# One step of a two-way recurrence: both directions through each stage together

## The chip, the cores and the metric

The kernel runs on one core of a Trainium2 chip. The metric is the device time of one execution in microseconds. Before the change it is 4082.77 us, the median of three runs (4077.72 to 4091.49).

PE is the matmul engine, PEld its weight loads, DVE the vector engine, ACT the scalar engine, POOL the GpSimd engine and SP the engine that issues most DMAs. Each engine runs its instructions in the order in which they stand in its queue.

## What is computed

One encoder layer over 2304 tokens (256 of a prompt and 2048 of a sample, width 1024): a norm, one input projection, then side by side a recurrent head group (RWKV-7, 8 heads of width 64, run forwards and backwards) and an attention group (8 query heads on 2 key/value heads), an output projection, a SwiGLU FFN and a last norm, all in 32-bit floats. The part that matters here is the recurrence. With a state S of 64x64 per head it is, per token:

```python
def step(S, inp):
    r_t, w_t, k_t, v_t, a_t, b_t = inp
    sa = jnp.einsum('bhvk,bhk->bhv', S, a_t)
    S = S * w_t[:, :, None, :] + sa[..., None] * b_t[:, :, None, :] + v_t[..., None] * k_t[:, :, None, :]
    return S, jnp.einsum('bhvk,bhk->bhv', S, r_t)
```

It is run once in the order of the tokens and once against it (`reverse=True`), with decay and gates of their own, and the two outputs are added and normalised per head.

## The kernel before

The tokens are cut into 36 chunks of 64. Within a chunk the recurrence is turned into matrix products; only the state passes from chunk to chunk. The forward direction (d = 0) takes the chunks upwards while the backward one (d = 1) takes them downwards, so one *step* of the scan treats two chunks, one per direction. There are 36 steps: 32 for the sample, 4 for the prompt.

A step has two parts, written as generators.

`scan_prep` (L626) loads a chunk's operands, forms the Gram products (L657) in two PSUM tiles of tag `g` (there are two such banks), masks them into `cl` and `mrb` on DVE (L661, L663), and transposes `bk` (L668) with an eviction on ACT (L669).

`scan_chain` (L686) is the serial part of one direction and one chunk. Its four stages write one half, `hb[:, d]`, of a single PSUM bank `hb`:
- first stage (L705): product of `cl` with `sv`, which holds state and v; ACT evicts it into `ry` (L707);
- second stage (L711): product with the inverse `x`; ACT evicts it in two copies into `sav` (L712, L713);
- third stage (L717): the change of the state; DVE adds the old state (L720) and multiplies by the decay `wc` (L722); then `scan_sv` copies the new state into the next `sv`, one half on ACT (L681), one on POOL (L682);
- fourth stage (L730, L733): the output product, into the same half of `hb`. In the first half of the steps ACT copies it out (L737) and a DMA stores it; in the second half DVE adds the stored output of the other direction (L746), and every second chunk `scan_out` normalises a tile of 128 tokens.

`scan` (L794) starts the preparation of the next step together with the chains of this one and takes a turn of each generator in every round. In the rounds it also advances the triangular inverses (`back`), and `build` advances attention by 2.75 units per round (`RATE_S`). A unit of attention is a score product (L880, L881) with its maximum on DVE (L882) and exponential on ACT (L884), or four transposes (L913) with evictions on ACT and DVE (L175, L181) and two products with the values (L916, L917). POOL multiplies the exponentials by their factors (L901), sixteen tiles in a row, each time that all scores of a tile of queries are there.

The text gives priorities, not the order: a scheduler places each instruction in its engine's queue when, by its own timeline, the operands and a buffer are ready, those earlier in the text first. So the queue of PE holds the chain's groups of eight heads between attention's products, and which stand next to each other is not written anywhere in the code. Two PE instructions are issued for each product of 32-bit operands in the chain, so eight heads are sixteen instructions. A product of attention that is 512 wide is one.

`e_dir` (L463 to L467), which runs before the scan, stores the decay at the end of each chunk in `wc[d]`, at the chunk's own number.

Of the kernel before, what the change touches and what calls it, by code (L numbers as in the profile page):

```python
# [8 lines left out]
F32 = mybir.dt.float32  # L9
# [8 lines left out]
P = 128  # L18
# [78 lines left out]
class Kern:  # L97
# [308 lines left out]
    def e_dir(self, e, p, d):  # L406
# [52 lines left out]
        for c in range(nch):  # L459
            for h in range(2):  # L460
# [5 lines left out]
        pool.tensor_scalar(out=self.wc[d][:, p, ch0:ch0 + nch], in0=e1[:, :nch, 64 - 64 * d], scalar1=1.0, scalar2=0.0,  # L466
                           op0=ALU.mult, op1=ALU.add)  # L467
# [156 lines left out]
    def scan_prep(self, d, c, sb, ps):  # L624

        nc = self.nc  # L626
        act, dve = nc.scalar, nc.vector
        bi, j = self.blk(c)
        gr, off = BLOCKS[bi][2:]
        cs = slice(j * P, j * P + P)  # L630
        q_ = self.sq = getattr(self, "sq", {})

        def T(tag, shape, bufs):
            return sb.tile(shape, F32, name=tag, tag=tag, bufs=bufs)
        ar = self.ard[d][bi]
        cl = T("cl", [P, 2, 4, P], 4)
        for e in range(2):
            rows = slice(e * 64, e * 64 + 64)
            self.ld(cl[rows, e], ar[:, rows, cs].rearrange("q p t -> p q t"))
        bk = T("bk_", [P, 4, P], 2)  # L640
        self.ld(bk, self.bkd[d][bi][:, :, cs].rearrange("q p t -> p q t"))
        x = T("x_", [P, 4, C], 3)
        for e in range(2):
            self.ld(x[e * 64:e * 64 + 64], self.xd[d][gr][:, e, off + j].rearrange("q s t -> s q t"))
        sav = T("sav", [P, 4, 2, C], 3)
        v = self.vtd[bi][j * C:(j + 1) * C, :]
        self.ld(sav[64:128].rearrange("p q e c -> p (q e c)"), v)
        gm = self.c["gmask_" + "fb"[d]]
        mrb = T("mrb", [C, 4, 2, C], 4)
        bkt = T("bkt", [P, 4, P], 3)  # L650
        q_[d, c] = dict(cl=cl, x=x, sav=sav, mrb=mrb, bkt=bkt, v=v.rearrange("t (q e c) -> t q e c", e=2, c=C))
        yield
        psgs = [ps.tile([P, 4, P], F32, name="g", tag="g", bufs=2) for _ in range(2)]
        for q in range(4):
            for e in range(2):
                rows = slice(e * 64, e * 64 + 64)
                nc.tensor.matmul(psgs[e][:, q, :], bk[rows, q, :], cl[rows, e, q, :], start=True, stop=True)  # L657
        for e in range(2):
            other = slice(64 - e * 64, 128 - e * 64)
            psg = psgs[e]  # L660
            dve.tensor_tensor(out=cl[other, e], in0=psg[64:128], op=ALU.mult,  # L661
                              in1=gm[64:128].rearrange("p (o t) -> p o t", o=1).broadcast_to([64, 4, P]))
            dve.tensor_tensor(out=mrb[:, :, e, :], in0=psg[0:64, :, 64:128], op=ALU.mult,  # L663
                              in1=gm[0:64, 64:128].rearrange("p (o t) -> p o t", o=1).broadcast_to([64, 4, C]))
            yield
        psg = ps.tile([P, 4, P], F32, name="g", tag="g", bufs=2)
        for q in range(4):
            nc.tensor.transpose(psg[:, q, :], bk[:, q, :], self.ident)  # L668
        act.copy(out=bkt, in_=psg)  # L669
        yield  # L670

    def scan_sv(self, d, c, st, sb):

        sv = sb.tile([P, 4, 2, C], F32, name="sv", tag=f"sv{d}", bufs=2)
        v = self.sq[d, c]["v"]
        self.ld(sv[64:128, :, 0, :], v[:, :, 0, :])
        self.ld(sv[0:64, :, 1, :], v[:, :, 1, :])
        if st[0] is None:
            st[0] = sb.tile([P, 4, C], F32, name="sc", tag=f"sc{d}", bufs=2)
            self.nc.gpsimd.memset(st[0], 0.0)  # L680
        self.nc.scalar.copy(out=sv[0:64, :, 0, :], in_=st[0][0:64])  # L681
        self.nc.gpsimd.tensor_scalar(out=sv[64:128, :, 1, :], in0=st[0][64:128], scalar1=1.0, scalar2=0.0, op0=ALU.mult,  # L682
                                     op1=ALU.add)
        st[1] = sv

    def scan_chain(self, d, c, nxt, st, first, sb, ps):  # L686
# [3 lines left out]
        o = self.sq[d, c]  # L690
        cl, x, sav, mrb, bkt = (o[k] for k in ("cl", "x", "sav", "mrb", "bkt"))

        def T(tag, shape, bufs):
            return sb.tile(shape, F32, name=tag, tag=tag, bufs=bufs)
        if st[1] is None:
            self.scan_sv(d, c, st, sb)
        sv = st[1]
        heads = [(h // 2, h % 2, slice(h % 2 * 64, h % 2 * 64 + 64)) for h in range(8)]

        
        def H():
            return self.hb[:, d]
        psa = H()
        for q, e, rows in heads:
            nc.tensor.matmul(psa[rows, q, :], cl[:, e, q, 0:64], sv[:, q, e, :], start=True, stop=True)  # L705
        ry = T("ry", [P, 4, C], 2)
        act.copy(out=ry, in_=psa)  # L707
        yield
        psx = H()
        for q, e, rows in heads:  # L710
            nc.tensor.matmul(psx[rows, q, :], x[rows, q, :], ry[rows, q, :], start=True, stop=True)  # L711
        act.copy(out=sav[0:64, :, 0, :], in_=psx[0:64])  # L712
        act.copy(out=sav[0:64, :, 1, :], in_=psx[64:128])  # L713
        yield
        pss = H()
# [684 lines left out]
```

## Time and profile before

| | |
|---|---|
| median of three runs | 4082.77 us |
| profiled execution, its own time | 4076.95 us |
| its span | 4074.8 us |
| PE busy | 3880.8 us, 95% |
| DVE busy | 2866.1 us, 70% |
| ACT busy | 2005.5 us, 49% |
| POOL busy | 1257.7 us, 31% |
| scan, first product of the chain to the last | 1015.0 to 2221.8 us |

Busy time is the time in which an engine executes something. PE's matmuls are pipelined, so a row of the time line for PE gives the start of a group, the time to the end of its last matmul, and the number of instructions; the pace is read from one start to the next. In brackets a row names how long the engine was idle before it, and what ended that; "issue" means that nothing in the profile explains it.

### The profile page before, as it was taken

How to read it: one execution, taken by the hardware profiler on the slowest of the kernel's cores; microseconds unless marked ns; L12 is line 12 of the kernel's file. 1: busy time of each engine (PE TensorE's matmuls, PEld its weight loads, DVE VectorE, ACT ScalarE, POOL GpSimd, SP SyncE). 2: the span in 40 equal slices, each digit the busy share in tenths (PEclk: the TensorE clock that was granted, in tenths of full speed). 3: DMA queues.
4: the chain of work that ended last, by engine and by line, in shares of the span. 5: the costliest groups of instructions: out<-in, count | busy, mean ns of one | idle time of the engine just before them, and what ended most of it. 6: DMA issues, size and time to landing. Idle time of an engine off the chain costs nothing.

```text
span 4074.8 us, 71176 instructions
## 1 busy us (share of the span) xinstructions
PE 3880.8 (95%) x26208; PEld 3336.7 (82%) x26208; DVE 2866.1 (70%) x4553; ACT 2005.5 (49%) x3940; POOL 1257.7 (31%) x1776
## 2 busy tenths in 40 slices
PE   8999999979999999999999889999989999999998
PEld 7987878746777777777777689998889988799987
DVE  5478586899889776898887577754477744577643
ACT  4345444456666655656666344443344433344432
POOL 2245353543223556734433122200122200212100
PEclk9999999979999999999999999999999999999999
DMA  6567566662433455444441423243423253422251
GB/s 200 166 204 228 173 207 192 207 165 59 101 74 86 92 120 118 114 109 104 109 111 43 146 86 104 96 181 109 166 93 104 96 184 110 159 87 96 102 181 67
DMA packets 646876, 524.32 MB, mean 129 GB/s; under 512 B 368512, under 2 KB 555520, under 8 KB 646528
## 3 DMA queue, kind: packets, MB, share of 16 engines
q1 hardware_dynamic: 577264, 438.36, 36.2%
q0 software_dynamic: 16944, 68.43, 5.1%
q10 hardware_dynamic: 52320, 12.98, 1.5%
q8 instruction: 207, 3.39, 0.3%
q14 instruction: 141, 1.16, 0.1%
HBM read 355.59 MB, written 166.37 MB: 128 GB/s over the span
## 4 chain that ended last, share of the span: by engine, by line
PE 76%; DVE 9%; DMA 4%; POOL 4%; issue 3%; ACT 3%; SPq 1%; ACTq 0%; DVEq 0%; POOLq 0%
PE acc L1082 23%; PE acc L211 8%; PE acc L212 8%; PE acc L213 8%; PE at L913 5%; PE g L657 3%; PE ao L917 3%; PE ao L916 3%; PE as L880 3%; PE as L881 2%; DVE nm L882 1%; DVE ptl L181 1%; PE hb L705 1%; PE hb L730 1%; PE g L597 1%
## 5 line engine op out<-in xcount | busy, mean ns | idle before, releaser
L1082 PE MATMUL acc<-H,wsh 128*128 128x384 f32 x3168 | 814.6, 337 | 32.6 <-ACT cg L1110 23.0
L1082 PEld LDWEIGHTS acc<-H,wsh 128*128 128x128 f32 x3168 | 578.7, 190 | 36.2 <-ACT cg L1110 24.1
L1082 PE MATMUL acc<-H,wsl 128*128 128x384 f32 x1584 | 533.2, 337 | 0.0
L901 POOL TENSOR_SCALAR p<-p,f 128x512 f32<-128x512 f32 (+1 forms) x528 | 372.8, 728 | 284.8 <-DVE f L897 235.9
L884 ACT ACTIVATE p<-as,nm 128x512 f32<-128x512 f32 (+1 forms) x528 | 360.9, 684 | 162.4 <-DVE nm L882 133.8
L211 PE MATMUL acc<-wsh,H 128*128 128x512 f32 x1080 | 419.8, 391 | 14.6 <-ACT wsh L175 14.6
L212 PE MATMUL acc<-wsl,H 128*128 128x512 f32 x1080 | 420.6, 390 | 0.0
L213 PE MATMUL acc<-wsh,H 128*128 128x512 f32 x1080 | 415.6, 389 | 0.0
L175 ACT CAST pth<-at 128x512 fp32r<-128x512 f32 x520 | 300.1, 586 | 228.7 <-PE at L913 223.2
L181 DVE TENSOR_TENSOR ptl<-at,pth 128x512 fp32r<-128x512 f32 x520 | 353.4, 683 | 75.8 <-ACT pth L175 73.4
L882 DVE TENSOR_REDUCE nm<-as 128x1 f32<-128x512 f32 (+1 forms) x528 | 353.0, 674 | 75.2 <-PE as L881 72.7
L211 PE MATMUL acc<-hThi,wih 128*128 128x384 f32 x1008 | 351.5, 349 | 0.8 <-ACT hThi L175 0.7
L212 PE MATMUL acc<-hTlo,wih 128*128 128x384 f32 x1008 | 348.5, 346 | 0.0
L213 PE MATMUL acc<-hThi,wil 128*128 128x384 f32 x1008 | 348.3, 345 | 0.0
L913 PE MATMUL at<-ident,p 128*128 128x128 f32 x2080 | 326.5, 277 | 2.9 <-POOL p L901 2.5
L913 PEld LDWEIGHTS at<-ident,p 128*128 128x128 f32 x2080 | 262.3, 142 | 68.2 <-POOL p L901 6.1
L181 DVE TENSOR_TENSOR wsl<-wsr,wsh 128x1024 fp32r<-128x1024 f32 x156 | 190.9, 1224 | 170.8 <-ACT wsh L175 170.7
L175 ACT CAST wsh<-wsr 128x1024 fp32r<-128x1024 f32 x156 | 164.1, 1052 | 297.9 <-PE acc L1082 151.8
L1082 PEld LDWEIGHTS acc<-H,wsl 128*128 128x128 f32 x1584 | 300.4, 190 | 0.0
L1025 POOL TENSOR_TENSOR sw<-wsr 128x512 f32<-128x512 f32 x66 | 89.2, 1352 | 643.8 <-DVE wsl L181 552.8
L880 PE MATMUL as<-kh,qs 128*128 128x512 f32 (+1 forms) x528 | 248.4, 471 | 31.8 <-ACT p L884 25.6
L181 DVE TENSOR_TENSOR wsl<-sw,wsh 128x1024 fp32r<-128x1024 f32 x132 | 161.2, 1221 | 138.3 <-ACT wsh L175 138.1
(661 smaller groups left out, 8375.1 us busy)
## 6 DMA issues: line engine op xcount, KB each, us to landing
wsr<-in_ffn_gate SPq DMA_DIRECT2D x66, 512.0 KB, 3.5
wsr<-in_ffn_up SPq DMA_DIRECT2D x66, 512.0 KB, 3.8
wsr<-in_ffn_down SPq DMA_DIRECT2D x66, 512.0 KB, 3.6
wir<-in_w_in POOLq DMA_DIRECT2D x63, 512.0 KB, 4.5
hd<-hid POOLq DMA_DIRECT2D x66, 384.0 KB, 3.8
H<-hd SPq DMA_DIRECT2D x33, 768.0 KB, 6.0
cl<-ard SPq DMA_DIRECT2D x144, 128.0 KB, 2.9
zT<-z SPq DMA_DIRECT2D x84, 192.0 KB, 2.7
```

The source lines that it names most:

```text
L175: nc.scalar.copy(out=hi, in_=src)
L181: e.tensor_tensor(out=lo, in0=src, in1=hi.bitcast(F32), op=ALU.subtract)
L211: mm(out, ahi, bhi, start=first, stop=False)
L212: mm(out, ahi, blo, start=False, stop=False)
L213: mm(out, alo, bhi, start=False, stop=last)
L657: nc.tensor.matmul(psgs[e][:, q, :], bk[rows, q, :], cl[rows, e, q, :], start=True, stop=True)
L880: nc.tensor.matmul(pss[:, :hw], qs[:, h, :], kh, start=True, stop=False)
L882: dve.tensor_reduce(out=nm[:, h, i:i + 1], in_=pss[:, :hw], axis=AX.X, op=ALU.max, negate=True)
L884: act.activation(out=p_[:, :hw], in_=pss[:, :hw], func=AF.Exp, bias=nm[:, h, i:i + 1], accum_out=ls[:, h, i:i + 1])
L901: pool.tensor_scalar(out=t, in0=t, scalar1=f[:, h, i:i + 1], scalar2=1.0, op0=ALU.mult, op1=ALU.mult)
L913: nc.tensor.transpose(tp[:, h, :], pt[h, i][:, k * P:(k + 1) * P], self.ident)
L1082: nc.tensor.matmul(acc, x[l][:, k, :], y_[r][:, k, :], start=first and k == 0 and i == 0, stop=k == 3 and i == 2, skip_group_check=True)
```

## The change

Both directions pass through each stage together. `scan_prep` and `scan_chain` now treat a step: sixteen heads per stage, one eviction over 512 columns in place of two over 256, one state tile for both directions. The whole bank `hb` holds one stage of both directions. The output product follows the update of the state directly, in a bank of tag `g` of its own, and no longer in `hb`. The decays of the backward direction are stored in reversed order, so that one column holds both directions' decays of a step. The generator of a chain has three turns in place of four; the preparation handles direction 0 in its second turn and direction 1 in its third. The core of the diff:

```diff
-    def scan_prep(self, d, c, sb, ps):
+    def scan_prep(self, step, sb, ps):
...
-        x = T("x_", [P, 4, C], 3)
...
-        sav = T("sav", [P, 4, 2, C], 3)
...
-        mrb = T("mrb", [C, 4, 2, C], 4)
-        bkt = T("bkt", [P, 4, P], 3)
...
+        sav = T("sav", [P, 2, 4, 2, C], 2)
+        mrb = T("mrb", [C, 2, 4, 2, C], 2)
...
+        for d in range(2):
+            bk, cl = bks[d], o["cl"][d]
+            gm = self.c["gmask_" + "fb"[d]]
+            psgs = [ps.tile([P, 4, P], F32, name="g", tag="g", bufs=2) for _ in range(2)]
+            for q in range(4):
+                for e in range(2):
+                    rows = slice(e * 64, e * 64 + 64)
+                    nc.tensor.matmul(psgs[e][:, q, :], bk[rows, q, :], cl[rows, e, q, :], start=True, stop=True)
...
-    def scan_chain(self, d, c, nxt, st, first, sb, ps):
+    def scan_chain(self, step, nxt, sb, ps):
...
-        heads = [(h // 2, h % 2, slice(h % 2 * 64, h % 2 * 64 + 64)) for h in range(8)]
...
+        heads = [(d, h // 2, h % 2, slice(h % 2 * 64, h % 2 * 64 + 64)) for d in range(2) for h in range(8)]
+        hb = self.hb
+
+        for d, q, e, rows in heads:
+            nc.tensor.matmul(hb[rows, d, q, :], cl[d][:, e, q, 0:64], sv[:, d, q, e, :], start=True, stop=True)
+        ry = T("ry", [P, 2, 4, C], 1)
+        act.copy(out=ry, in_=hb)
+        yield
+        for d, q, e, rows in heads:
+            nc.tensor.matmul(hb[rows, d, q, :], x[d][rows, q, :], ry[rows, d, q, :], start=True, stop=True)
+        sg = sav.rearrange("p d q e c -> p (d q) e c")
+        act.copy(out=sg[0:64, :, 0, :], in_=hb[0:64].rearrange(f))
+        act.copy(out=sg[0:64, :, 1, :], in_=hb[64:128].rearrange(f))
+        yield
+        for d, q, e, rows in heads:
+            nc.tensor.matmul(hb[rows, d, q, :], bkt[d][:, q, rows], sav[:, d, q, e, :], start=True, stop=True)
+
+        t = T("st", [P, 2, 4, C], 1)
+        dve.tensor_tensor(out=t, in0=hb, in1=st[0], op=ALU.add)
+        sc = T("sc", [P, 2, 4, C], 2)
+        dve.tensor_tensor(out=sc.rearrange(f), in0=t.rearrange(f), op=ALU.mult, in1=self.wc[:, :, :, step["at"]:step["at"] + 1]
+                          .rearrange("p d q o -> p (d q) o").broadcast_to([P, 8, C]))
         st[0] = sc
+        psy = ps.tile([P, 2, 4, C], F32, name="g", tag="g", bufs=2)
...
         if nxt is not None:
-            self.scan_sv(d, nxt, st, sb)
-        yield
-        psy = H()
...
+            self.scan_sv(nxt, st, sb)
...
-                for d, c, st, first in steps[k - 1]:
-                    nxt = steps[k][d][1] if k < len(steps) and steps[k][d][2] is st else None
-                    gens.append(self.scan_chain(d, c, nxt, st, first, sb, ps))
-                gens = gens[-2:] + gens[:-2]
+                nxt = steps[k] if k < len(steps) and steps[k]["st"] is steps[k - 1]["st"] else None
+                gens.insert(0, self.scan_chain(steps[k - 1], nxt, sb, ps))
```

The lines of the chain are L719 (first stage), L724, L730 (third), L741 and L744 (output) after the change; L893, L894, L926, L929 and L930 are attention's products, L665 the Gram products.

The instructions' order moves on PE. The first place is the third stage of the sixteenth step (`hb<-sav,bkt`), with the products of attention around it (`as`, `ao`) and its transposes (`at`). Before, on PE:

```order
L869 MATMUL as<-ident,qdup 128x128 x4
L717 MATMUL hb<-sav,bkt 64x64 x8
L917 MATMUL ao<-ptl,vst_8787 128x512
L916 MATMUL ao<-pth,vst_8787 128x512
L913 MATMUL at<-ident,p 128x128 x4
L917 MATMUL ao<-ptl,vst_8787 128x512
L913 MATMUL at<-ident,p 128x128 x4
L717 MATMUL hb<-sav,bkt 64x64 x8
L880 MATMUL as<-kh_18412,qs 128x512
```

After, on PE, the same stage:

```order
L730 MATMUL hb<-sav,bkt 64x64
L893 MATMUL as<-kh_8784,qs 128x512
L894 MATMUL as<-kl_8785,qs 128x512
L730 MATMUL hb<-sav,bkt 64x64 x2
L929 MATMUL ao<-pth,vst_8759 128x512
L730 MATMUL hb<-sav,bkt 64x64 x5
L930 MATMUL ao<-ptl,vst_8759 128x512
L926 MATMUL at<-ident,p 128x128 x4
L893 MATMUL as<-kh_8784,qs 128x512
L929 MATMUL ao<-pth,vst_8759 128x512
L894 MATMUL as<-kl_8785,qs 128x512
L730 MATMUL hb<-sav,bkt 64x64 x2
```

The two groups of eight heads stood whole before; now ten of the sixteen heads stand here in four pieces, and the other six follow in two more.

The second place is the way on PE from the third stage of the tenth step to the first stage of the eleventh (`hb<-sv,cl`). Before, from the second direction's third stage, the first 12 of 33 rows:

```order
L717 MATMUL hb<-sav,bkt 64x64 x8
L916 MATMUL ao<-pth,vst_8814 128x512
L917 MATMUL ao<-ptl,vst_8814 128x512
L916 MATMUL ao<-pth,vst_8833 128x512
L913 MATMUL at<-ident,p 128x128 x4
L880 MATMUL as<-kh_8831,qs 128x512
L881 MATMUL as<-kl_8832,qs 128x512
L917 MATMUL ao<-ptl,vst_8833 128x512
L913 MATMUL at<-ident,p 128x128 x4
L880 MATMUL as<-kh_8831,qs 128x512
L881 MATMUL as<-kl_8832,qs 128x512
L668 MATMUL g<-ident,bk__14710 128x128 x4
```

After, the whole way:

```order
L730 MATMUL hb<-sav,bkt 64x64 x16
L741 MATMUL g<-sv,cl 64x64 x16
L744 MATMUL g<-sav,mrb 64x64 x16
L665 MATMUL g<-cl,bk__14585 128x128 x4
L929 MATMUL ao<-pth,vst_8759 128x512
L930 MATMUL ao<-ptl,vst_8759 128x512
L926 MATMUL at<-ident,p 128x128 x4
L719 MATMUL hb<-sv,cl 64x64
```

The two output products, which came after further attention before, now follow at once and whole, and six rows stand between the third stage and the next first one.

## Rows read from the trace of the kernel before

**Rows 1.** page, span, and busy time of each engine (share of the span), instructions

```profile
span 4074.8 us, 71176 instructions
...
PE 3880.8 (95%) x26208; PEld 3336.7 (82%) x26208; DVE 2866.1 (70%) x4553; ACT 2005.5 (49%) x3940; POOL 1257.7 (31%) x1776
```

**Rows 2.** page, chain of work that ended last, by engine

```profile
PE 76%; DVE 9%; DMA 4%; POOL 4%; issue 3%; ACT 3%; SPq 1%; ACTq 0%; DVEq 0%; POOLq 0%
```

**Rows 3.** busy time by stretch, the scan

```profile
core 0: us, PE busy (x) PEld busy (x) DVE busy (x) ACT busy (x) POOL busy (x), PEclk, DMA share, GB/s
1015.00:2221.80 1206.80, 1164.56 (x11330) 921.69 (x11328) 995.34 (x1961) 751.64 (x1846) 529.14 (x831) 0.99 0.41 99
```

**Rows 4.** groups of the scan: xcount | busy us, mean ns | idle before

```profile
L901 POOL TENSOR_SCALAR p<-p,f 128x512 f32<-128x512 f32 (+1 forms) x432 | 303.5, 725 | 199.1 <-DVE f L897 157.4 <-DVE i L567 19.7 <-ACT pth L175 18.0
...
L705 PE MATMUL hb<-sv,cl 128*64 128x64 f32 x1152 | 55.1, 229 | 1.6 <-DVE yt L746 0.6 <-POOL sv L682 0.5 <-ACT ry L707 0.5
...
L669 ACT COPY bkt<-g 128x512 f32<-128x512 f32 x72 | 42.0, 587 | 7.4 <-PE g L668 7.1
...
L722 DVE TENSOR_TENSOR sc<-st,wc 128x256 f32<-128x256 f32 x72 | 36.8, 511 | 1.3
...
L720 DVE TENSOR_TENSOR st<-hb,sc 128x256 f32<-128x256 f32 x72 | 29.9, 415 | 3.2 <-PE hb L717 2.8
L682 POOL TENSOR_SCALAR sv<-sc 64x256 f32<-64x256 f32 x70 | 29.0, 414 | 297.5 <-DVE sc L722 168.2 <-PE as L881 41.0 <-PE ao L917 26.2
...
L707 ACT COPY ry<-hb 128x256 f32<-128x256 f32 x72 | 26.9, 373 | 38.0 <-PE hb L705 36.3 <-DMA qdup<-qd 1.6
...
L765 DVE TENSOR_TENSOR yt<-yt,s 128x512 f32<-128x512 f32 x17 | 12.3, 724 | 1.5 <-POOL s L764 1.4
```

**Rows 5.** time line of PE, an uncut block: start us, us to end, instructions

```profile
1444.91 0.69 PE L717 MATMUL hb<-sav,bkt 128*64 128x64 f32 x16
1445.53 0.50 PE L917 MATMUL ao<-ptl,vst 128*128 128x512 f32 x1
1445.86 0.40 PE L880 MATMUL as<-kh,qs 128*128 128x512 f32 x1
1446.10 0.40 PE L881 MATMUL as<-kl,qs 128*128 128x512 f32 x1
```

**Rows 6.** time line of PE, a block in pieces

```profile
2214.11 0.50 PE L916 MATMUL ao<-pth,vst 128*128 128x512 f32 x1
2214.54 0.33 PE L733 MATMUL hb<-sav,mrb 64*64 64x64 f32 x4
2214.80 0.50 PE L880 MATMUL as<-kh,qs 128*128 128x512 f32 x1
2215.14 0.40 PE L881 MATMUL as<-kl,qs 128*128 128x512 f32 x1
2215.38 0.40 PE L917 MATMUL ao<-ptl,vst 128*128 128x512 f32 x1
```

**Rows 7.** time line of the weight loader at the same place

```profile
2214.53 0.19 PEld L733 LDWEIGHTS hb<-sav,mrb 64*64 64x64 f32 x4 [0.24 <-issue]
...
2216.14 0.19 PEld L733 LDWEIGHTS hb<-sav,mrb 64*64 64x64 f32 x4 [0.17 <-issue]
```

**Rows 8.** waits of PE in the scan stretch: us in total, times, longest us

```profile
PE as L880 <- ACT p L884: 16.2, 21, 1.6
...
PE g L657 <- DMA cl<-ard: 4.7, 7, 1.0
```

**Rows 9.** time line of POOL, normalisations and copies of the state

```profile
1319.22 6.08 POOL L901 TENSOR_SCALAR p<-p,f 128x512 f32<-128x512 f32 x8
1325.39 0.41 POOL L682 TENSOR_SCALAR sv<-sc 64x256 f32<-64x256 f32 x1
...
1342.34 10.74 POOL L901 TENSOR_SCALAR p<-p,f 128x512 f32<-128x512 f32 x16 [2.64 <-DVE f L897]
```

**Rows 10.** time line of PE, a first stage at that place

```profile
1325.85 0.68 PE L705 MATMUL hb<-sv,cl 128*64 128x64 f32 x14 [0.54 <-POOL sv L682]
```

More of the change, by code (lines that the diff above doesn't have):

```diff
@@ L655, in scan_prep @@
+        sav = T("sav", [P, 2, 4, 2, C], 2)
+        mrb = T("mrb", [C, 2, 4, 2, C], 2)
+        o = self.sq[step["c"]] = dict(sav=sav, mrb=mrb, cl=[], x=[], bkt=[], v=[])
+        bks = []
+        for d, c in enumerate(step["c"]):
+            bi, j = self.blk(c)
+            gr, off = BLOCKS[bi][2:]
+            cs = slice(j * P, j * P + P)
+            cl = T("cl", [P, 2, 4, P], 4)
             for e in range(2):
                 rows = slice(e * 64, e * 64 + 64)
-                nc.tensor.matmul(psgs[e][:, q, :], bk[rows, q, :], cl[rows, e, q, :], start=True, stop=True)
@@ L658, in scan_prep @@
[L658 to L664, printed above, removed]
-            yield
@@ L666, in scan_prep @@
[L666 to L669, printed above, removed]
-        yield
[L672 to L677, printed above, removed]
+                self.ld(cl[rows, e], self.ard[d][bi][:, rows, cs].rearrange("q p t -> p q t"))
@@ new lines, in scan_prep, with scan_sv @@
+        for d in range(2):
+            psg = ps.tile([P, 4, P], F32, name="g", tag="g", bufs=2)
+            for q in range(4):
+                nc.tensor.transpose(psg[:, q, :], bks[d][:, q, :], self.ident)
+            bkt = T("bkt", [P, 4, P], 3)
+            act.copy(out=bkt, in_=psg)
+            o["bkt"].append(bkt)
+        yield
+    def scan_sv(self, step, st, sb):
+        sv = sb.tile([P, 2, 4, 2, C], F32, name="sv", tag="sv", bufs=2)
+        for d, v in enumerate(self.sq[step["c"]]["v"]):
+            self.ld(sv[64:128, d, :, 0, :], v[:, :, 0, :])
+            self.ld(sv[0:64, d, :, 1, :], v[:, :, 1, :])
@@ L695, in scan_chain @@
         if st[1] is None:
-            self.scan_sv(d, c, st, sb)
+            self.sq[step["c"]] = o
+            self.scan_sv(step, st, sb)
+            del self.sq[step["c"]]
         sv = st[1]
-        heads = [(h // 2, h % 2, slice(h % 2 * 64, h % 2 * 64 + 64)) for h in range(8)]
[L701 to L706, printed above, removed]
@@ L707, in scan_chain @@
-        act.copy(out=ry, in_=psa)
-        yield
[L709 to L713, printed above, removed]
-        yield
-        pss = H()
-        for q, e, rows in heads:
-            nc.tensor.matmul(pss[rows, q, :], bkt[:, q, rows], sav[:, q, e, :], start=True, stop=True)
-        t = T("st", [P, 4, C], 1)
```

117 lines of the change are left out of this document (60 added, 57 removed).

## Prediction, before the run

> **What bounds the kernel now.** I read the page first. PE is busy 95% of the span [rows 1] and carries 76% of the chain that ended last [rows 2]. The change touches only the scan (and one small copy before it), so the next view is the table by stretch. From the first product of the chain to the last, 1015.0 to 2221.8 us, PE is busy 1164.56 of 1206.80 us, so 42 us are idle, while DVE has 211 us, ACT 455 us and POOL 678 us to spare [rows 3]. There are 36 steps, so a step lasts 33.5 us and holds 32.3 us of PE work, the chain's own and that of the attention which runs beside it. The latency of the chain, which the change shortens, is not what a step's length comes from. A clock term is left out: the granted clock in that stretch is 0.99 of the 2.4 GHz level [rows 3].
>
> So the question is what PE's row of work costs after the change, and how much of its 42 idle us comes or goes.
>
> **The evictions and copies.** ACT issues 162 copies fewer, DVE 72 operations fewer, POOL 38 fewer (counted from the instructions of each engine in both programs). Two copies of 256 columns cost 2 x 0.373 us; one of 512 columns costs 0.587 [rows 4]: 162 x 0.159 = 26 us less on ACT. On DVE, 36 pairs of 0.415 and 36 of 0.511 become 72 operations near 0.724 (a 128x512 one with a broadcast operand) [rows 4]: 36 x (0.830 + 1.022 - 1.448) = 15 us less. The POOL copies go from 0.414 to about 0.725, half as many [rows 4], which is nothing. None of these engines ends the wait in the scan, so I count all of it at zero directly, hidden under 1165 us of PE. What it can do is shorten the times at which attention's products wait for ACT: 16.2 us in 21 waits [rows 8]. A little of that will go. Its bounds are 0 and the whole idle time of PE, 42 us; I take 10, nearer to the row, as the rest of the idle time is spread over waits for DVE and DMA that stay.
>
> **PE's own row.** The number of matmuls is the same. What moves is their order. Before, the third stage is always eight heads of one direction, never interrupted; after, sixteen heads of both are one block in the text, but the order cuts them up, first in the fifth step and in most from the twelfth on (the first place shown with the change: pieces of 1, 2, 5 and 2 heads with attention between). I counted over PE's rows from the first of the chain to the last product of attention. The pieces in which chain, preparation and inverse stand go from 671 to 836 (first stage 90 to 150, third 72 to 100, preparation's Gram products 126 to 169). The returns from such a piece to attention's products go from 410 to 541, and the entries into one from a 512-wide product from 249 to 352. The preparation is cut because the output product now holds one of the two g banks that its eight matmuls alternate between.
>
> The price of a piece comes from two places of the trace. Uncut, sixteen instructions take 1444.91 to 1445.53, 0.62 us; the first 512-wide product behind them takes 0.33 to the next one, the following one 0.24 [rows 5]. Cut, a 512-wide product needs 0.43 until a piece can follow (2214.11 to 2214.54), the piece of four instructions 0.26, the next product 0.34, and then it is 0.24 again [rows 6]. Four instructions of an uncut block are worth 0.62 x 4/16 = 0.155. One extra piece thus costs (0.43 - 0.24) + (0.26 - 0.155) + (0.34 - 0.24) = 0.39 us; 0.24 of it shows as idle of the weight loader, put down to issue [rows 7]. A piece that is entered from transposes has only the last two terms, 0.20. With 103 pieces at 0.39 and 28 at 0.20 the sum is 40 + 6 = **46 us more on PE**. Bounds: 131 x 0.20 = 26, and all 165 further pieces at 0.39 = 64.
>
> The Trainium skill ("TensorE: Matmul & The Clock Gate", section "Step-by-step: what each phase is for") says that PE takes weight loads out of order, ahead of matmuls still running, when their row groups don't collide or the spare weight buffer is the target. By that rule a switch to other weights would be free and the term above would be 0. The trace does not agree here: the loads before the pieces start 0.17 to 0.24 us after the loader went idle [rows 7].
>
> **Cover of the chain.** Before, the two directions stood apart: one direction's eviction and state update ran under the other's matmuls. At the second place shown, 31 rows of other work stood between the end of a step's third stage and the next step's first, and 6 stand there now. At the pace of the rows that is some 4.4 us of PE work now (product 4 x 0.61, half a block of the preparation, two 512-wide products, four transposes); over all steps I get about 6 as median, and 15 before. In this time the state must be added (about 0.7) and scaled (0.72), and copied (ACT 0.6, POOL 0.73, side by side): 2.2 us if no queue is full. So the usual step is covered, with 2 to 4 us left. The exception is POOL: sv's second half stands in its queue behind attention's normalisations, sixteen of which last 10.74 us, and once before the first stage already waited 0.54 us for it, after eight of them [rows 9, 10]. In the order after, full blocks of sixteen stand right ahead of sv at 11 places. If each started when the state was ready, 10.74 + 0.73 - 3.8 = 7.7 us would be missing, 85 us in all; if each started 8 us before, nothing. The wait in the row was 0.54 us with a cover some 9 us longer, so I take 1 us at each, **10 us**, and half the upper end, 40, for the range.
>
> Everything behind the scan (the rest of attention, the FFN) has the same instructions in the same order on PE, and so has all ahead of it; the copy of the decay on POOL only writes to another place. DMAs keep their number; all loads of a step are now issued together, under the previous step's chain, and the waits for them were 4.7 us in the largest group [rows 8]. I change nothing there.
>
> **Sum.** 46 + 10 - 10 = 46 us on the profiled execution's 4076.95 us, whose span is 4074.8: 4123. The median of the runs is 4082.77, 0.14% above the profiled one, so the forecast is 4129 us, 1.1% slower.
>
> **Rivals.**
> - *The breaks are hidden: no change.* If the scheduler cuts a block where attention would have waited anyway, its cost stands in PE's idle 42 us, and 46 - 42 is 4: 4087 us. For it: the cuts stand between products whose operands come from ACT and DVE. Against it: only 16.2 us of PE's waits are for ACT in attention, the longest 1.6 us, in 21 places [rows 8], and there are 131 cuts. The Trainium skill ("Perfetto Trace Analysis", section "Identifying the Most-Contended Engine") wants PE judged by the busy share of weight loads, since matmul busy time hides headroom. By 921.69 of 1206.80 us [rows 3] that would be 76%, room enough for this case; I hold against it that the idle time of the loader is just what the switches make.
> - *Fewer waits: faster.* The joint evictions take 26 us off ACT and the product's own bank ends the wait of the next first stage for the product's eviction. If the cuts are hidden as above and half of the idle 42 us goes too, the result is 4083 - 21 = 4062 us. It decides if PE's idle time in the scan falls below 25 us while its busy time stays at 1165. Against it: the chain's stages hardly made PE wait before (all releasers of the first stage on PE together 1.6 us [rows 4]), so there is little to take.
> - *The cover fails: much slower.* The sv copies or the joint copies come late at most steps: 46 + 40 = 86 us, 4169 us. For it: the shorter distance in the order. Against it: the distances still exceed the sum of the durations at the usual step.
>
> **Chances and range.** A measurement of this kernel tells 0.3%, 12 us, from no change. Forecast 0.55, hidden 0.17, faster 0.13, cover fails 0.15. Slower is 0.55 + 0.15 less 0.01 for a forecast case that ends within 12 us: 0.69; no change 0.18; faster 0.13. For the range, the ends of the terms are 26 + 0 - 42 = -16 and 64 + 40 - 0 = 104 us, which gives 4067 to 4187; I cut the upper end to 4175, as both upper ends together are unlikely. The likeliest case alone reaches from 4102 to 4155.
>
> **What would show it.** Right: PE's busy time in the scan stretch up by some 45 us, groups of hb in pieces of two to twelve instructions with 512-wide products between, the loader's "issue" idle time ahead of the chain's lines up, ACT down by about 26 us and DVE by 15. Cover: PE's waits for sv on POOL up from 0.5 us to about 10. Wrong: if the idle time of PE fell by as much as its busy time rose, or if its busy time did not rise at all, which would mean that a cut costs nothing.

## The result

| | before | after |
|---|---|---|
| median of four runs each | 4086.59 us (4077.72 to 4091.49) | 4193.80 us (4185.12 to 4202.39) |
| profiled execution, its span | 4074.8 us | 4195.5 us |
| mean granted clock over the runs, share of 2.4 GHz | 0.974 | 0.968 |

A fourth run of the kernel before moved its median from 4082.77 to 4086.59. The clock of the kernel before is the mean of the 87 runs that were made beside the experiments.

The change makes the kernel slower: the ratio is 1.0261, 95% interval 1.0243 to 1.0279, or 107 us. The forecast was 4129 us, so the sign was right and the size was not: less than half of the loss was foreseen, and 4193.8 lies above the range, and above the 4187 that its terms gave before the upper end was cut to 4175. No rival's time (4087, 4062, 4169) was met either.

The page after, span and engines, to be read against [rows 1]:

```profile
span 4195.5 us, 70717 instructions
...
PE 3988.1 (95%) x26208; PEld 3389.1 (81%) x26208; DVE 2865.7 (68%) x4481; ACT 1994.6 (48%) x3778; POOL 1251.5 (30%) x1738
```

The instruction counts of DVE, ACT and POOL fall by the 72, 162 and 38 that were counted from the order. PE has the same 26208 matmuls and is busy 107 us longer. Outside the stretch from the chain's first product to the last of attention, PE's rows are the same in both programs by line and shape. The table by stretch: first of before from the chain's first product to attention's last (scan and the rest of attention), then of after the scan alone, which answers to [rows 3], and the same whole stretch.

```profile
1015.00:2281.50 1266.50, 1216.56 (x11586) 958.10 (x11584) 1038.48 (x2039) 786.89 (x1922) 557.06 (x870) 0.99 0.40 95
```

```profile
1014.00:2328.50 1314.50, 1259.69 (x11247) 964.18 (x11245) 979.43 (x1866) 729.06 (x1652) 518.27 (x794) 0.96 0.38 91
1014.00:2403.50 1389.50, 1325.69 (x11587) 1011.64 (x11585) 1036.61 (x1968) 777.46 (x1760) 546.28 (x834) 0.96 0.36 87
```

The whole stretch is 123 us longer: PE is busy 109 us more and idle 14 us more (63.8 against 49.9). So the loss is PE's own row of work, not the chain's latency. The stretch holds the same work in both programs; over it the durations of ACT's instructions add up to 27 us less and those of DVE's to 13 us less, which gave nothing. (Their busy time in the table, in which instructions that overlap count once, falls by 9 and 2 us.) The granted clock of the stretch falls from 0.99 to 0.96.

**Where blocks are cut.** The time line of PE after, the third stage of the fifteenth step, the one before the step that is shown with the change (start us, us to the end, instructions), and the loader at the same place:

```profile
1509.27 0.69 PE L730 MATMUL hb<-sav,bkt 128*64 128x64 f32 x16
1509.89 0.49 PE L929 MATMUL ao<-pth,vst 128*128 128x512 f32 x1
1510.31 0.45 PE L730 MATMUL hb<-sav,bkt 128*64 128x64 f32 x6
1510.69 0.50 PE L930 MATMUL ao<-ptl,vst 128*128 128x512 f32 x1
1511.02 0.60 PE L926 MATMUL at<-ident,p 128*128 128x128 f32 x4
...
1511.92 0.40 PE L929 MATMUL ao<-pth,vst 128*128 128x512 f32 x1
1512.25 0.56 PE L730 MATMUL hb<-sav,bkt 128*64 128x64 f32 x10
```

```profile
1510.31 0.31 PEld L730 LDWEIGHTS hb<-sav,bkt 128*64 128x64 f32 x6 [0.24 <-issue]
...
1512.25 0.42 PEld L730 LDWEIGHTS hb<-sav,bkt 128*64 128x64 f32 x10 [0.37 <-issue]
```

The product ahead of the piece takes 0.42 us (1509.89 to 1510.31), the one behind it 0.33, and the loader is idle ahead of both pieces, as in [rows 6, 7]. The columns to compare in these rows are the two numbers in "128*64" and "128*128": the part of the array that an instruction uses. It differs between chain and attention, so a switch of work is a switch of that too. The Trainium skill ("TensorEngine Tiling (Array Packing)", section "Key Properties") says that changing the tiling mode drains the engine. These rows agree with it, and it was the rule to weigh, rather than that of the loads pulled ahead. That the loader's idle time is such a drain is not shown by a run of its own.

The loader's groups over the scan, first before, then after (xcount | busy, mean ns | idle before):

```profile
L705 PEld LDWEIGHTS hb<-sv,cl 128*64 128x64 f32 x1152 | 42.5, 137 | 23.0 <-issue 14.0 <-ACT pth L175 1.4 <-DVE yt L746 1.0
L733 PEld LDWEIGHTS hb<-sav,mrb 64*64 64x64 f32 x1152 | 41.7, 136 | 7.4 <-issue 1.5
L730 PEld LDWEIGHTS hb<-sv,cl 128*64 128x64 f32 x1152 | 40.8, 139 | 19.4 <-issue 8.1 <-DVE ptl L181 2.4 <-DVE sc L722 1.6
L717 PEld LDWEIGHTS hb<-sav,bkt 128*64 128x64 f32 x1152 | 39.8, 138 | 18.3 <-issue 7.8 <-DVE sc L722 1.8 <-DVE st L720 1.4
```

```profile
L719 PEld LDWEIGHTS hb<-sv,cl 128*64 128x64 f32 x1152 | 52.2, 140 | 35.7 <-issue 24.2 <-DVE nm L895 2.1 <-ACT pth L175 2.0
L741 PEld LDWEIGHTS g<-sv,cl 128*64 128x64 f32 x1152 | 44.1, 141 | 15.4 <-issue 13.0 <-PE ao L929 0.4 <-PE as L894 0.4
L730 PEld LDWEIGHTS hb<-sav,bkt 128*64 128x64 f32 x1152 | 44.1, 137 | 21.8 <-issue 19.8 <-ACT p L897 0.3 <-ACT kh L175 0.2
L744 PEld LDWEIGHTS g<-sav,mrb 64*64 64x64 f32 x1152 | 43.5, 136 | 15.1 <-issue 12.5 <-ACT pth L175 0.2
```

These four groups (first stage, third stage, and the output product's two parts) held 31.4 us of "issue" before and hold 69.5 after.

**The groups and waits** that answer to [rows 4, 8, 10]:

```profile
L719 PE MATMUL hb<-sv,cl 128*64 128x64 f32 x1152 | 73.1, 236 | 0.5 <-ACT sv L694 0.5
L735 DVE TENSOR_TENSOR sc<-st,wc 128x512 f32<-128x512 f32 x36 | 28.8, 801 | 1.1 <-DVE st L733 0.5
L733 DVE TENSOR_TENSOR st<-hb,sc 128x512 f32<-128x512 f32 x36 | 24.6, 683 | 7.4 <-PE hb L730 7.3
L695 POOL TENSOR_SCALAR sv<-sc 64x512 f32<-64x512 f32 x35 | 22.0, 630 | 347.6 <-DVE sc L735 143.7 <-PE at L926 56.5 <-DVE f L905 35.7
L721 ACT COPY ry<-hb 128x512 f32<-128x512 f32 x36 | 21.4, 594 | 9.1 <-PE hb L719 9.0
```

```profile
PE as L893 <- ACT p L897: 18.5, 27, 2.2
PE g L600 <- DMA i<-xpt: 6.5, 3, 3.1
...
PE g L665 <- DMA bk__12164<-bkd: 3.1, 1, 3.1
...
PE g L665 <- DMA bk__21525<-bkd: 2.6, 1, 2.6
```

The joint operations cost about what was read off (scaling on DVE 0.80 us where 0.72 was taken, the copy on POOL 0.63 where 0.73 was). The first stage waits for `sv` 0.5 us in all, and not for POOL: the cover held. Attention's waits for ACT did not shrink (16.2 to 18.5 us), and there are single waits of 2.6 to 3.1 us for loads, where the longest for a load was 1.7 before.

**The clock.** One such wait and what follows it, and two waits ahead of another stretch (PE after), then three stretches (column PEclk):

```profile
1626.64 0.60 PE L926 MATMUL at<-ident,p 128*128 128x128 f32 x4
1630.30 1.71 PE L600 MATMUL g<-i,i 32*128 32x128 f32 x8 [3.06 <-DMA i<-xpt]
...
1632.95 1.06 PE L926 MATMUL at<-ident,p 128*128 128x128 f32 x4
1633.66 0.78 PE L929 MATMUL ao<-pth,vst 128*128 128x512 f32 x1
...
1646.78 0.60 PE L926 MATMUL at<-ident,p 128*128 128x128 f32 x4
1647.13 0.48 PE L930 MATMUL ao<-ptl,vst 128*128 128x512 f32 x1
...
1669.85 0.50 PE L893 MATMUL as<-kh,qs 128*128 128x512 f32 x1 [0.99 <-ACT p L897]
...
1671.63 0.78 PE L893 MATMUL as<-kh,qs 128*128 128x512 f32 x1 [1.05 <-ACT p L897]
```

```profile
1630.60:1644.40 13.80, 13.80 (x57) 12.02 (x55) 4.36 (x7) 3.42 (x7) 1.10 (x2) 0.51 0.28 50
1644.40:1655.00 10.60, 10.60 (x74) 9.26 (x74) 6.67 (x12) 4.14 (x11) 2.81 (x8) 1.00 0.24 50
1671.70:1695.60 23.90, 20.45 (x86) 13.60 (x88) 16.89 (x30) 10.01 (x25) 18.06 (x25) 0.50 0.28 70
```

After 3.06 us of idling PE runs at 0.5, the 1.2 GHz level, for 13.8 us, and four transposes take 0.71 us instead of 0.35. Busy time hides this: PE counts as busy throughout. In the stretch the profile after has 119.5 us at that level, the one before 37.5. After, it falls into fourteen pieces. Waits for a load (1.2 to 3.2 us) stand ahead of five of them, 44 us together; the longest, 23.9 us, has attention's waits for ACT of 0.99 and 1.05 us ahead of it, and most others have such waits for ACT or DVE, up to 2.2 us.

Here a single profile misleads, since the share differs from run to run. The mean granted clock over the runs is 0.9738 before (87 runs) and 0.9683 after (4): at 2 x (1 - clock) of the span that is 214 and 266 us at the half level per execution, 52 us more. If work takes double there, that is an estimated **26 us of the 107**, good to some 4 us, as the four clocks after lie between 0.966 and 0.970. Of the profile's 123 us the same reckoning gives 41 to the clock; PE stood idle for 11 of the 119.5 us and 2 of the 37.5, so 41 is an upper estimate. Both leave some 81 us at full clock.

### The profile page after: what moved, and what is told of

The parts are those of the page before. It is cut to its first block, busy times and chain, and to the rows that moved or that the text cites. A ratio compares the mean times of both kernels' runs of the same rounds, so it can differ in the third digit from the quotient of the medians.

```text
span 4195.5 us, 70717 instructions
## 1 busy us (share of the span) xinstructions
PE 3988.1 (95%) x26208; PEld 3389.1 (81%) x26208; DVE 2865.7 (68%) x4481; ACT 1994.6 (48%) x3778; POOL 1251.5 (30%) x1738
## 4 chain that ended last, share of the span: by engine, by line
PE 61%; DVE 4%; POOL 1%; issue 1%; ACT 1%; DMA 1%; SPq 1%; ACTq 0%; POOLq 0%; DVEq 0%
PE acc L1095 22%; PE acc L211 6%; PE acc L213 6%; PE acc L212 6%; PE at L926 3%; PE g L665 3%; PE ao L930 2%; PE ao L929 2%; PE as L893 2%; PE as L894 2%; PE hb L719 1%; PE hb L724 1%; PE g L741 1%; PE hb L730 1%; PE g L744 1%
## 5 line engine op out<-in xcount | busy, mean ns | idle before, releaser
L926 PE MATMUL at<-ident,p 128*128 128x128 f32 x2080 | 328.0, 278 | 6.0 <-DVE ptl L181 3.1
L926 PEld LDWEIGHTS at<-ident,p 128*128 128x128 f32 x2080 | 262.3, 143 | 70.6 <-POOL p L914 6.9
L893 PE MATMUL as<-kh,qs 128*128 128x512 f32 (+1 forms) x528 | 258.0, 489 | 37.5 <-ACT p L897 28.7
```

The lines of the kernel that those rows point to most:

```text
L893: nc.tensor.matmul(pss[:, :hw], qs[:, h, :], kh, start=True, stop=False)
L926: nc.tensor.transpose(tp[:, h, :], pt[h, i][:, k * P:(k + 1) * P], self.ident)
```

## Experiments

Theory A says that the cuts in PE's order cost the time, theory B that the joint stages or the product's bank do. After e4 theory A2 takes A and adds a price for the bank, paid at the Gram products; later theory L names the late loads of `bk`. In the table "returns" are those from a piece of chain or preparation to attention's products, counted in PE's order as in the prediction; busy and idle are PE's in the profile, over the whole stretch; the clock is the mean over the runs. Ratios are to the kernel before, run on the same chip each time (its median lay between 4084.8 and 4094.6).

| | returns | median us | ratio, 95% interval | busy, idle us | clock |
|---|---|---|---|---|---|
| before | 410 | 4086.6 | | 1216.6, 49.9 | 0.974 |
| after | 541 | 4193.8 | 1.0261 (1.0243 to 1.0279) | 1325.7, 63.8 | 0.968 |
| e1 whole | 358 | 4103.5 | 1.0032 (1.0016 to 1.0047) | 1225.3, 64.8 | 0.972 |
| e2 rate | 266 | 4109.2 | 1.0046 (1.0031 to 1.0061) | 1215.6, 75.8 | 0.973 |
| e3 joint only | 558 | 4158.4 | 1.0174 (1.0157 to 1.0191) | 1304.7, 51.9 | 0.970 |
| e4 product only | 411 | 4132.9 | 1.0105 (1.0090 to 1.0120) | 1258.6, 59.2 | 0.973 |
| e5 whole, hb | 358 | 4091.2 | 1.0016 (1.0005 to 1.0027) | 1205.6, 71.9 | 0.970 |
| e6 Gram by half | 417 | 4097.1 | 1.0027 (1.0014 to 1.0040) | 1239.3, 45.2 | 0.973 |
| e7 Gram paired | 373 | 4044.8 | 0.9905 (0.9886 to 0.9923) | 1173.6, 54.7 | 0.976 |
| e8 whole, paired | 274 | 4087.5 | 0.9997 (0.9984 to 1.0011) | 1175.8, 85.9 | 0.971 |
| e9 before, cut | 548 | 4149.4 | 1.0145 (1.0121 to 1.0169) | 1276.1, 42.1 | 0.970 |
| e10 after, paired | 314 | 4088.8 | 1.0000 (0.9984 to 1.0016) | 1199.7, 73.0 | 0.973 |
| e11 product, paired | 352 | 4093.7 | 1.0022 (1.0006 to 1.0039) | 1206.5, 69.2 | 0.972 |
| e12 e10, rate 2.25 | 263 | 4080.1 | 0.9979 (0.9967 to 0.9991) | 1183.4, 80.1 | 0.973 |
| e13 e8, product in hb | 340 | 4091.6 | 1.0014 (0.9997 to 1.0030) | 1191.2, 83.7 | 0.969 |
| e14 e11, bk x4 | 383 | 4072.3 | 0.9971 (0.9956 to 0.9985) | 1201.0, 54.8 | 0.975 |
| e15 e12, bk x3 | 264 | 4061.3 | 0.9941 (0.9923 to 0.9960) | 1177.2, 66.5 | 0.974 |
| e16 after, bk x3 | 613 | 4236.0 | 1.0353 (1.0335 to 1.0371) | 1346.4, 52.5 | 0.970 |

### Are the cuts the cause? e1, e2, e9

e1 is the changed kernel. Each of the five groups of chain products gets the first line of this edit; the tie (`keep_in_program_order`) is on the first half of the output product alone, which is the group shown:

```diff
+        with self.tc.high_priority(offset=4000):
             for d, q, e, rows in heads:
-                nc.tensor.matmul(psy[rows, d, q, :], cl[d][:, e, q, 64:128], ...)
+                mm = nc.tensor.matmul(psy[rows, d, q, :], cl[d][:, e, q, 64:128], ...)
+                self.tc.keep_in_program_order(mm)
```

> The changed kernel with the chain's five groups of products given precedence over attention's, and the output product's first half tied behind the third stage, so that groups stay whole: in PE's order the returns from a piece to attention's products fall from 541 to 358 (410 in the kernel before), the entries from a 512-wide product from 352 to 223 (249 before). Joint evictions, the product's own bank, loads and buffers stay as they are after the change. Theory A (the cut blocks cost the time, and the further half-clock time follows from them): with pairs of PE's instructions at the paces of the trace before, this order is some 24 us shorter than the order before, so 4045 to 4100 us, at or below the kernel before. Theory B (the joint stages or the product's place in a g bank cost it, whatever the order): 4165 us or more. Theory C (the clock drops come from waits for the step's loads, which are all issued at once with fewer buffers, and not from the cuts): half-clock time in the scan stays near 119 us and the time lies between, 4120 to 4165 us.

Measured 4103.5: 90 of the 107 us are gone with everything else of the change in place. That is 4 us above theory A's window and far from B's.

e2, also the changed kernel:

```diff
-RATE_E, RATE_S = 1.0, 2.75
+RATE_E, RATE_S = 1.0, 2.0
```

> The changed kernel with only the number of attention units written per round of the scan lowered from 2.75 to 2.0. The text of attention then lies behind the chain's, the chain has precedence by its place in the text, and its groups stay nearly whole: returns 541 to 266, entries from 512-wide products 352 to 161. 92 units of attention's scores are left behind the scan (28 after the change as it was). Theory A (cuts): the order is some 98 us shorter than after the change at the paces of the trace before, 36 us below the kernel before: 4040 to 4085 us. Theory B (joint stages or g bank): 4165 us or more. A third reading, that attention alone behind the scan can't keep PE fed, gives 4100 us or more with the waits standing behind the last product of the chain.

4109.2: B falls again, but A's upper bound is missed by 24 us. PE is busy as long as before, and idle 26 us more. Part of the third reading holds: the shorter order was paid for with waits of attention that no chain covers.

e9 is the kernel before, the five groups with the opposite sign:

```diff
+        with self.tc.high_priority(offset=-1500):
             for q, e, rows in heads:
                 nc.tensor.matmul(psa[rows, q, :], cl[:, e, q, 0:64], sv[:, q, e, :], start=True, stop=True)
```

> The kernel before with one thing changed: the chain's five groups are given a lower precedence than attention's products, so that its groups of eight heads are cut as after the change: returns 410 to 548, entries from 512-wide products 249 to 338, pieces 671 to 763. Stages stay apart, the output product stays in hb, Gram products stand whole in 24 groups (26 before). Theory A2 (the cuts cost by themselves): some 38 us by the paces of PE's pairs in the trace before, and further half-clock time, 4115 to 4165 us. Rival (cuts cost only in the joint form, by the chain's length): 4080 to 4105 us.

4149.4, as theory A2 has it: 62 us (49 to 69 by the interval) from precedence alone, with nothing joint. Its two parts, up to attention's last product and behind it:

```profile
1022.90:2280.00 1257.10, 1226.17 (x10945) 946.84 (x10944) 1019.31 (x1987) 775.64 (x1888) 547.49 (x857) 0.99 0.38 91
2280.00:2341.00 61.00, 49.88 (x633) 42.37 (x632) 21.76 (x42) 13.68 (x33) 2.54 (x7) 0.69 0.51 156
```

The cut part runs at 0.99; what half-clock time the stretch has more lies in a tail in which the chain is alone. So theory A's addition, that half-clock time follows from the cuts, falls. The prediction's price, 89 more entries at 0.39 and 49 more returns at 0.20, gives 44.5 us here. The clock over the runs (0.970) takes an estimated 16 of the 62 us, which leaves 46, some 10 either way. A second count agrees: the numbers "128*128", "128*64" and so on change from one PE instruction to the next 936 times in the stretch before, and 1216 times both after and in e9. With half of what PE is busy at the half level taken off, its busy time in the stretch is 49 us longer in e9 than before, and 72 us in the changed kernel. So some 24 us of the changed kernel's busy time need another cause than the switches.

### Which half of the change? e3, e4, e5

e3 keeps the joint stages and puts the product back:

```diff
-        psy = ps.tile([P, 2, 4, C], F32, name="g", tag="g", bufs=2)
+        if nxt is not None:
+            self.scan_sv(nxt, st, sb)
+        yield
+        psy = hb
```

> Only one part of the change: both directions pass each stage together with joint evictions, but the output product stays in the bank hb and a turn later, as before the change. Returns 558 and entries 364 in this order, hardly fewer than after the change (541, 352). Theory A: what cuts the blocks is joining them, so this is slower than before by 40 to 90 us, 4125 to 4175. Rival: the product's own bank, which takes one of the two g banks from the preparation, is what costs the time; then this one lies at 4080 to 4110 us.

e4 is the kernel before with the product moved alone:

```diff
-            self.scan_sv(d, nxt, st, sb)
-        yield
-        psy = H()
+        psy = ps.tile([P, 4, P], F32, name="g", tag="g", bufs=2)[:, :, 0:64]
...
+            self.scan_sv(d, nxt, st, sb)
```

> Only the other part: directions apart as before the change, the output product right behind the state's update in a g bank. Returns 411 and entries 264 (410 and 249 before). Theory A: 4080 to 4110 us, near the kernel before. Rival (the g bank costs the time): 4140 us or more.

4158.4 and 4132.9: 71 and 46 us. e3 is as theory A says. e4 lies between both windows and speaks against theory A alone: as many returns as before, and still 46 us. Both halves cost; that their sum of 117 is near the 107 need not mean that they add up.

e5 is e3 with the precedence of e1:

> The joint stages of e3 (product in hb, a turn later) with the precedence of e1, so that blocks stay whole (returns 358, entries 219). It differs from e1 only in where the output product stands. Theory A2 (two causes: joining the directions leads to the cuts; the product's g bank costs some 40 us more, since the Gram products lose one of their two banks and no longer alternate between the two halves of the rows, and since bk's buffers come free later): 4055 to 4080 us, 25 to 45 below e1. Rival (e1's remaining 16 us over before are half-clock time that joint stages bring wherever the product stands): 4095 to 4110 us.

4091.2, 12 us below e1: between the two, nearer the rival. The price of the bank in the joint form is 12 us where blocks are whole, not 25 to 45; where they are cut it is 35 us (e3 to after).

### What the bank takes: e6, e7, e8, e10, e11

The Gram products (L657) use one half of the rows each, the lower for e = 0 and the upper for e = 1, and write a bank per e. A piece of eight instructions of one bank before, and a whole group of sixteen in e7 (PE):

```profile
1461.72 1.16 PE L657 MATMUL g<-cl,bk__16201 64*128 64x128 f32 x8
1462.80 0.50 PE L916 MATMUL ao<-pth,vst 128*128 128x512 f32 x1
```

```profile
1493.59 1.16 PE L657 MATMUL g<-cl,bk__16703 64*128 64x128 f32 x16
1494.68 0.50 PE L918 MATMUL ao<-pth,vst 128*128 128x512 f32 x1
```

Eight take 1.08 us and sixteen 1.09: where the halves alternate, two products run side by side, and the second starts 6 or 7 ns behind the first instead of some 110. Before, 27 of the 72 groups stood in one piece of 14 or 16 instructions; after, 7. Of the 1152 Gram instructions, those that start within 30 ns of the one ahead are 150 before and 87 after. Moving the output product from `hb` to a g bank takes such starts away in each form: 150 to 87 with directions apart (before to e4), 195 to 87 with joint stages (e3 to after), 191 to 153 with whole blocks (e5 to e1). The mean distance of two Gram starts in the scan at full clock goes from 105 to 118 ns from before to after: 12 us over the 912 pairs after. The Trainium skill ("TensorE: Matmul & The Clock Gate", section "Why this matters for your kernels") says that matmuls in distinct row groups run concurrently; these rows agree.

e6 is before, with the loops over q and e exchanged; e7 is before, e8 is e1, e10 the changed kernel and e11 e4, each with this edit:

```diff
-                nc.tensor.matmul(psgs[e][:, q, :], bk[rows, q, :], cl[rows, e, q, :], start=True, stop=True)
+                mm = nc.tensor.matmul(psgs[e][:, q, :], bk[rows, q, :], cl[rows, e, q, :], start=True, stop=True)
+                if q + e:
+                    self.tc.keep_in_program_order(mm)
```

> The kernel before with one loop order changed: the eight Gram products of a chunk by row half (four of the lower half, then four of the upper) instead of alternating. Nothing else changes; returns 417 and entries 241 (410, 249). In the trace before, 26 of 72 groups stand whole and alternate; sixteen such instructions start within 1.21 us, two halves of eight within about 0.88 + 0.11 each and some more, so each group loses 0.5 to 0.8 us. Theory A2: 13 to 20 us more, 4098 to 4108 us. Rival (the alternation is worth nothing): 4081 to 4093 us.

> The kernel before with the opposite edit: the eight Gram products tied together in the order of the text, so that each group alternates between both halves of the rows and waits for both g banks. Nearly all 72 groups alternate instead of 26; the pieces go from 671 to 655, returns from 410 to 373, entries from 249 to 222. Theory A2: 46 groups by 0.5 to 0.8 us and some 10 to 16 us from fewer switches, 35 to 50 us less: 4040 to 4065 us. Rival (waiting for the second bank blocks PE's queue and costs as much as it gives): 4080 us or more.

> e1 (all of the change, blocks whole) with the Gram products tied in pairs as in e7. Returns 274, entries 192 (e1 358, 223). Theory A2: what the g bank took from the Gram products comes back and the switches fall too, 30 to 50 us below e1: 4050 to 4075 us, and below the kernel before. Rival (tied products wait for the bank that the output product holds): 4100 us or more, with PE waiting at the Gram products.

> The changed kernel with only the eight Gram products tied in pairs (the edit of e7). Besides alternating in nearly all groups, the order has fewer cuts: returns 541 to 314, entries 352 to 212. Theory A2: the switches give some 90 us back at the paces of the trace before and the pairing some 30; as e5 and e8 kept some 40 us of waits and half-clock time that the joint stages bring, 4075 to 4115 us. Rival (pairing costs waits for the bank that the output product holds): 4130 us or more.

> e4 (directions apart, output product early in a g bank) with the Gram products tied in pairs. Returns 352 (e4 411, e7 373), entries 232 (e4 264, e7 222). Theory A2 in its strict form (what e4 lost, it lost at the Gram products' pairing): within 20 us of e7, 4045 to 4065 us. Rival (the bank costs by other ways, above all bk's buffers that come free later and so later loads): 4080 us or more, with PE waiting for bk's loads.

e6 lost 11 us, just short of its window; it has 70 side-by-side starts where before has 150. e7 gained 41 as expected and beats both kernels; it has 442 such starts, and the time from each Gram start at full clock to the next start, summed, fell from 131 to 98 us. e10, inside A2's window: one edit takes 105 us off the changed kernel, by pairing and by the fewer switches together. With that edit in both, the change still costs 44 us (e10 against e7). e8 (4087.5) missed its window on the upper side: its PE is as little busy as e7's, but idle 31 us more. e11 gained 39 us on e4 and still lies 49 above e7, so the strict form of A2 is wrong. It has 14.1 us of waits for bk's loads in 12 places, the longest of them:

```profile
PE g L657 <- DMA bk__20832<-bkd: 2.6, 1, 2.6
PE g L657 <- DMA bk__16717<-bkd: 2.4, 1, 2.4
PE g L657 <- DMA bk__11352<-bkd: 1.9, 1, 1.9
PE g L657 <- DMA bk__13277<-bkd: 1.8, 1, 1.8
```

### Late loads: e14, e16, and the rest: e12, e13, e15

e14 is e11 with four buffers for bk, as shown; e16 is the changed kernel and e15 is e12 with three (to make room, both have three buffers for x in place of four and one for the small tile `s1` in place of two). e12 is e10 at a rate of 2.25; e13 is e5 with the edit of e7:

```diff
-            bk = T("bk_", [P, 4, P], 2)
+            bk = T("bk_", [P, 4, P], 4)
```

> e11 (directions apart, product early in a g bank, Gram products paired) with four buffers for bk in place of two, so that its loads no longer wait for the transposes of the chunk before. The order has somewhat more switches (returns 383, e11 352; 17 us more at the paces of the trace before). Theory L (late loads of bk: 14 us of waits in 12 places and the half-clock time that follows them): waits for bk gone, half-clock time down from 75 to 40 us or less, 4065 to 4090 us in spite of the switches. Rival: 4095 to 4115 us.

> The changed kernel with three buffers for bk in place of two (and three for x in place of four, to make room); nothing else. The order is cut more: returns 541 to 613, entries 352 to 398, some 26 us more at the paces of the trace before. Theory L (the half-clock time follows PE's long waits, those for bk's loads above all): the waits for bk are gone and the half-clock time falls from 119.5 to 75 us or less, which gives 20 to 40 us back, 4175 to 4205 us. Rival (cuts and joint stages bring it): half-clock time stays at 110 us or more, 4210 to 4235 us.

> e10 with 2.25 attention units per round in place of 2.75: returns 263 (e10 314), entries 189 (212), 21 units of scores left behind the scan (25). Theory A2: 10 to 25 us below e10. Rival (fewer cuts leave attention's own waits uncovered, which take the gain back): as e10 or above it.

> e8 (joint stages, blocks whole, Gram products paired) with the output product in hb and a turn later, so no g bank is taken. Returns 340, entries 206 (e8 274, 192); 62 units of scores left behind the scan (e8 32). Theory G (what e8 lacks against e7, 43 us, is the price of the product's g bank, as e11 against e7): 4045 to 4065 us. Rival J (joint stages cost it themselves, by waits of attention that whole blocks leave uncovered, and the half-clock time behind them): 4075 to 4095 us.

> e12 (the change with paired Gram products and 2.25 units per round) with three buffers for bk and, to make room, three for x. Returns 264, entries 176 (e12 263, 189). Theory L: 4060 to 4078 us, below e12. Rival (bk's loads make PE wait only 3.6 us in e12, so nothing is to be had there): within 8 us of e12's 4080.

e14: 4072.3, inside theory L's window. No wait for bk's loads is left; the Gram products' one wait for a load is for `cl`:

```profile
PE g L657 <- DMA cl<-ard: 1.1, 1, 1.1
```

The clock rises from 0.972 to 0.975, although the switches grew. So with directions apart, late loads are 21 of the 49 us that e11 lies above e7 (by the expectation's estimate of 17 us for the further switches, up to 38). The other 28, up to e7's 4044.8, stay open.

e16: 4236.0, past both windows. No wait for bk is left and the profiled execution has only 51 us at half clock, but it was the quickest of four (clock 0.975; the others 0.966 to 0.969). Over the runs the clock is 0.970, hardly above the 0.968 of after, and the 72 further returns cost. So theory L is not shown for the changed kernel.

e12 gained 9 us on e10, just short of the 10 expected, and 0.2% on the kernel before. e13 supports the rival: without the bank's part the joint form is no faster than e8, and PE idles as long (83.7 us against 85.9). So the idle time that e8 has over e7 does not come from the bank. The bank's own price is not read from this pair, since e13 has 66 more returns. e15: 4061.3, inside theory L's window, 0.6% below the kernel before and the best joint version; its PE is busy as long as in e7 and idle 12 us more. Its gain over e12 is larger than the rival's 8 us, but e12's waits for bk were only 3.6 us, so the loads alone don't explain it.

Alternating both halves of the rows within one bank was not tried.

## Why the prediction was right and wrong

- **What bounds it, and the sign: right.** The chain's latency and the evictions never mattered; the 26 us less on ACT and 15 on DVE were there as sums of durations (27 and 13) and bought nothing.
- **The price of a switch: right.** The 46 us are borne out by e9 (46 measured net of the clock, 44.5 by the prices); so close a match is partly luck, as the measured figure is good to some 10 us. "Hidden" is refuted: idle time did not fall.
- **"A clock term is left out": the step that failed first.** It was left out because the clock stood at 0.99, as if it stayed so. In the changed kernel it stood at 0.96, which cost an estimated 26 us over the runs. What lowers it is open. Waits for loads stand ahead of 44 of the 119.5 us at the half level. With directions apart, e14 supports them as a cause (without waits for bk the clock rose from 0.972 to 0.975, ten runs each); for the changed kernel e16 doesn't, and the longest piece stands behind attention's waits for ACT.
- **The Gram products: under-sized.** That the bank cuts them was seen; it was priced as switches only. The loss of the partner in the other half of the rows, 12 us, is a term of its own, and e7 gained 41 us on the kernel before by tying them in pairs.
- **Relief -10: wrong sign.** PE's idle time rose by 14 us, and attention's waits for ACT from 16.2 to 18.5.
- **Cover +10: did not come.** The waits for `sv` were 0.5 us, none of them for POOL.

46 + 26 + 12 + 14 = 98 of 107 us; 9 stay unassigned. The sum is an estimate, as 26 is from the runs and 12 and 14 are from the profiles. That precedence by place in the text is enough to cut the blocks, e9 shows, and e1 shows that giving the chain precedence undoes it. That in the changed kernel the faster chain runs ahead of attention's text, so that each ready product of attention goes first, is argued and not shown; e2 fits it (266 returns with less attention written per round). Open is why the joint form with whole, paired blocks (e8, e13) idles some 30 us more than e7; e2 suggests that whole blocks leave attention's own waits uncovered.

## What to carry to other kernels

Where one engine is the bound, read a change from what it does to the neighbours in that engine's queue: count the switches between kinds of work and price them from start to start, and count the pairs that could have run side by side. A freed wait elsewhere is worth nothing there, and a PSUM bank given to one product is taken from another (in e4, 63 of 150 side-by-side starts went with it). Compare the granted clock over several runs, not over one profile, before a clock term is sized or left out.

## What the runs showed of the hardware

Sixteen Gram instructions that alternate between the two halves of the rows took 1.09 us, eight of one half 1.08. At the 1.2 GHz level four transposes took 0.71 us instead of 0.35, in a stretch in which PE shows no idle time at all. The same program's mean clock varied between 0.966 and 0.975 from run to run (e16), with times from 4240 to 4218 us.
